# Small products in turn by array tile, the two heads of an attention pair in turn, and the latent keys of both heads in one product

## The chip, the cores and the metric

One Trainium2 chip, one core of it. The time is the device time of one execution in microseconds; lower is better. The core has a matrix engine (TensorE, PE in the profile, with its weight loads as PEld), a vector engine (VectorE, DVE), a scalar engine (ScalarE, ACT), GpSimd (POOL) and SyncE (SP), which issues the DMAs.

## What is computed

A two-layer backbone over 512 latent tokens and 256 context tokens, 1024 wide. In each layer a normalised and modulated stream goes through one input projection whose columns feed three groups of heads; their outputs are joined and projected back, and a SwiGLU block follows. Cut to what the change touches:

```python
# latent attention, 4 heads: keys and values from a 128-wide latent, a shared rotary part appended to each key
kv = (rms_norm(kvc, g_kv) @ w_kv_up).reshape(..., MLA_H, MLA_NOPE + MLA_V)
keys, vals = concat([ck, k]), concat([cv, v])        # context and latent tokens
out = softmax(q @ keys.T * scale) @ vals

# neighbourhood attention, 4 heads of 64, on an 8 x 64 grid, 16 columns around each query, and the context
p = softmax(concat([where(col_ok, q @ k_window.T * scale + bias, -inf), q @ ck.T * scale]))
o = p_loc @ v_window + p_ctx @ cv

# gated DeltaNet, 4 heads, two directions, chunks of 64: a unit lower triangular inverse per chunk and head
tinv = triangular_solve(L + eye, eye, lower=True, unit_diagonal=True)
u, w = tinv @ (v * beta), tinv @ (kb * exp(gc))
S_new = S * g_last + k_tail.T @ (u - w @ S)
```

## The kernel before, in words

All products are on TensorE. A product that has to be as good as fp32 at speed is split into a high and a low part and done as three products (`mm3`, line 107); other products take fp32 operands as they are, and the profile records each of those as two passes, a weight load and a matmul for each. `mm` (line 103, the call of the engine at line 104) is the one place from which nearly every product comes, so L104 says nothing about which it is; the names of the tiles do. The profile shortens names of tiles: pp64 is pp there, yq64 is yq, p32 and p64 are p, and Ys is strips.

The program is written as a sequence, and a framework puts each engine's instructions in an order of its own: ready work of several streams is interleaved on each engine, and the engine then runs its list in that order. Program order is the priority. Tiles come from rotating buffers: asking for a new one waits until the oldest of its tag has been read.

**Inverses.** `inverse(x0, sb, eb)` (line 916) makes the inverses for two chunks of 128 tokens, eight (chunk, head) pairs x. 32x32 blocks on the diagonal come ready from an earlier stage; the function joins them to 64x64 and then to 128x128. It has five groups of small products: pp (four 32-blocks b, eight x each; 32 products of 32x32, input mix), xq (blocks 1 and 2; 16 products of 32x32, input p), pp64 (two halves, 16 products of 64x64, input X), yq (32 products of 32x32, input strips), and yq64 (two halves, 16 products of 64x64, input Y). Block b lies on partitions 32b to 32b+31, which are rows of the array; its result goes to the partitions of block b^1 of one PSUM bank, or of b itself in xq. In each group the loop over blocks or halves is outside, that over x inside. There are three calls per layer: `inverse(0)` beside the last input projections, `I_(2)` and `I_(4)` as steps in the list `dn` beside the attentions.

**Neighbourhood attention.** `attention()` (line 847) is a generator; one `next` is one unit: a pair of heads and 128 queries. Layer 0 has 12 units (8 latent, 4 context), layer 1 has 8 latent ones. For each head j of the pair (its 64 dimensions on partitions 64j to 64j+63) a bank `s_` is taken, the scores of the window (256 columns, latent units only) and of the context (256 columns) are made with `mm3`, and then maximum (L870, L874), exponents (L877, L878), normalisation, four transposes (L889) and a copy (L891) follow. Then the value products of both heads fill one bank `o_`: for each block of 128 keys head 0, then head 1. The banks of tag S (scores) number two, those of tag T (transposes, values, accumulators) three.

**The list of steps beside it.** `beside()` (line 1099) takes steps from `dn` (scans and inverses) and, in layer 0, modulation columns from `ada_cols`, by the counts in `DNS` and `ADA`, before each unit of either attention; `TAIL` sets where the first units and the last projections stand. These lists are not changed.

**Latent attention.** For each pair of heads, head by head: query weights are loaded and split (`upw`, line 1138, one shared buffer wup), then the head's keys are made from 64 columns of `wkh`/`wkl` into bank `acc_mk`, 512 latent and 256 context columns, each evacuated by a cast (L1168, ACT) and a subtraction (L1169, DVE) into `kh`, `kl`; then its queries. Units of 128 queries follow, as in the neighbourhood attention; the value products (bank `o_mla`) go over the key blocks 0 to 5, for each of them head 0 and then head 1. The out-projection's first part is interleaved here by the framework.

Of the kernel before, what the change touches and what calls it, by code (L numbers as in the profile page):

```python
# [9 lines left out]
F32 = mybir.dt.float32  # L10
F32R = mybir.dt.float32r
AF = mybir.ActivationFunctionType
ALU = mybir.AluOpType
# [4 lines left out]
P = 128  # L18
# [344 lines left out]
def layer(tc, nc, a, l, es_x, xT, env, nx):  # L363
# [483 lines left out]
    def attention():  # L847
        for pair in range(2):
# [4 lines left out]
            for qt in range(nT // P):  # L853
# [5 lines left out]
                lo_ = 256 if is_ctx else 0  # L859
                pts = []  # L860
                for j in range(2):
                    hs = slice(64 * j, 64 * j + 64)
                    cutk = lambda t: grid(t)[hs, :, c0:c0 + 32].rearrange("p r (b c) -> p b r c", b=2)
                    s_ = att_bank("s_na")
                    if not is_ctx:
                        mm3(nc, s_[:, 0:256], (qh[hs, tok], ql[hs, tok]), (cutk(kh), cutk(kl)))
                    mm3(nc, s_[:, 256:512], (qh[hs, tok], ql[hs, tok]), (kh[hs, CTX], kl[hs, CTX]))
                    st_ = sn.tile([P, 8], F32, tag="st", name="st", bufs=4)
# [25 lines left out]
                for b in range(len(vb)):  # L894
                    for j in range(2):
                        hd = 2 * pair + j
                        mm(nc, o_[j * 64:j * 64 + 64, 0:P], nav[:, vb[b], hd * 64:hd * 64 + 64], pts[j][:, b * P:(b + 1) * P],
                           b == 0, b == len(vb) - 1)
# [17 lines left out]
    def inverse(x0, sb, eb):  # L916
# [14 lines left out]
        pp, xq = i8(q2[:, 0:256], 32), i8(q2[:, 256:512], 32)  # L931
        for b in range(4):
            o = b ^ 1
            for x in R8:
                mm(nc, pp[B4[o], x], LP[x // 4][B4[b], x % 4, B4[o]], mix[B4[b], x])
# [12 lines left out]
        S.copy(out=p32, in_=pp)  # L948
        for b in (1, 2):
            for x in R8:  # L950
                mm(nc, xq[B4[b], x], Ys[1 - b % 2][B4[b], x], p32[B4[b], x])
# [5 lines left out]
        hf = ((fst, snd), (snd, fst))  # L957
        for a_, b_ in hf:
            for x in R8:
                mm(nc, pp[b_, x], LP[x // 4][a_, x % 4, b_], Xh[a_, x])  # L960
# [3 lines left out]
        yq = i8(eb("yq")[:, 0:256], 32)  # L964
        for b in range(4):
            o = b ^ 1
            for x in R8:
                mm(nc, yq[B4[o], x], p32[B4[b], x], Ys[1 - b % 2][B4[b], x])
        for d, r, c in ((0, 0, 1), (0, 2, 3), (1, 1, 0), (1, 3, 2)):
            S.copy(out=Y[d][B4[r], :, c], in_=yq[B4[r]])  # L970
        yq = i8(eb("yq64"), 64)
        for d, (a_, b_) in enumerate(hf):
            for x in R8:
                mm(nc, yq[a_, x], p64[b_, x], Yf[d][b_, x, b_])
            S.copy(out=Yf[d][a_, :, b_], in_=yq[a_])
# [178 lines left out]
    for pair in range(2):  # L1154
        qk = []
        for j in range(2):
            hd = 2 * pair + j
            wqh, wql = upw(a["w_qup"][l, hd], 256, [(gq[:, i:i + 1], P * i, P * i + P) for i in range(2)], "wq")
            ws = slice(hd * 64, hd * 64 + 64)
            kh, kl = khl[j]  # L1160
            qh, ql = [sa.tile([P, T], F32R, tag=nm, name=nm, bufs=2) for nm in ("qh", "ql")]
            qf = sa.tile([P, T], F32, tag="pt", name="qf", bufs=2)
            q2 = sa.tile([P, T], F32, tag="pr", name="q2", bufs=2)
            for st_ in both:
                n = st_.stop - st_.start
                acc = att_bank("acc_mk")
                mm3(nc, acc[0:64, 0:n], (wkh[:, ws], wkl[:, ws]), (kvh[:, st_], kvl[:, st_]))
                S.copy(out=kh[0:64, st_], in_=acc[0:64, 0:n])  # L1168
                tt(out=kl[0:64, st_], in0=acc[0:64, 0:n], in1=kh[0:64, st_].bitcast(F32), op=ALU.subtract)  # L1169
            for st_ in sts:  # L1170
                n = st_.stop - st_.start
                acc = att_bank("acc_mq")
                for i in range(2):
                    w = slice(i * P, i * P + P)
                    mm3(nc, acc[:, 0:n], (wqh[:, w], wql[:, w]), (qll_[i][0][:, st_], qll_[i][1][:, st_]), i == 0, i == 1)
                S.copy(out=qf[0:64, st_], in_=acc[0:64, 0:n])
                tt(out=qf[64:96, st_], in0=acc[64:96, 0:n], in1=C("rope")[64:96, st_], op=ALU.mult)
                tt(out=q2[64:96, st_], in0=acc[96:128, 0:n], in1=C("rope")[96:128, st_], op=ALU.mult)
            dict(V=V, G=G)[next(eng, "G")].tensor_tensor(out=qf[64:96, :nT], in0=qf[64:96, :nT], in1=q2[64:96, :nT], op=ALU.add)
            split((qh[0:96, :nT], ql[0:96, :nT]), qf[0:96, :nT])  # L1180
            qk.append((kh, kl, qh, ql))
        for qt in range(nT // P):
# [38 lines left out]
            b0 = kst[0][1]  # L1221
            for b in range(b0, 6):
                for j in range(2):
                    hd = 2 * pair + j
                    mm(nc, o_[j * 64:j * 64 + 64, 0:P], vtok[:, b, hd * 64:hd * 64 + 64], pts[j][:, b * P:(b + 1) * P],
                       b == b0, b == 5)
            if pair:
# [239 lines left out]
```

## Time and profile before

| what | us |
|---|---|
| median of 3 runs | 2122.88 |
| lowest, highest | 2118.37, 2123.48 |
| profiled execution, its own time | 2125.45 |
| its span, first to last instruction | 2123.6 |
| TensorE's granted clock, mean | 0.968 |

The profile is of one execution. Busy time of an engine is the time covered by at least one of its instructions; matmuls are pipelined, so two records may overlap and a stream's records cover a little more than the time from its first start to its last. In a row of a timeline the first number is the start from the beginning of the span, the second the time covered, then engine, line, operation, out<-in, sizes and the number of records that were merged. For a matmul, 32*32 is the rows by columns of the array that it uses, 32x32 the partitions and columns that move.

### The profile page before, as it was taken

What the parts mean: (1) busy time and instruction counts of PE and PEld (TensorE: products, weight loads), DVE (VectorE), ACT (ScalarE), POOL (GpSimd) and SP (SyncE); (2) the same over time, 40 slices, a digit from 0 to 9 for tenths busy, and PEclk for the clock granted to TensorE, in tenths of its full rate; (3) what the DMA queues carried; (4) which work ended last, traced back from release to release, by engine and by line L of the source; (5) the groups of instructions that cost most, each with busy time, mean ns of one, the idle gap of its engine ahead of it and who ended that gap; (6) DMA issues with size and microseconds to landing.
All of it is one profiled execution on the core that took longest, in us unless ns stands there. A gap on an engine that the chain in (4) does not pass through costs nothing. (4 is left out here: it accounts for less than half of the span.)

```text
span 2123.6 us, 32023 instructions
## 1 busy us (share of the span) xinstructions
PE 1990.2 (94%) x12770; PEld 1684.4 (79%) x12770; DVE 1172.3 (55%) x2045; ACT 714.3 (34%) x1385; POOL 758.7 (36%) x540
## 2 busy tenths in 40 slices
PE   6999998998998999999999988888998889999998
PEld 4788787887787888888888876767787678888887
DVE  4888813667656457246443268894568753212123
ACT  5433322334544221122122244333434543222233
POOL 3466132104322222322222443823311353444444
PEclk9999998999999999999999999999999999999999
DMA  7324252543322345344442331334232231333332
GB/s 279 82 76 153 81 157 77 168 149 112 104 64 78 109 126 165 97 130 131 128 129 76 121 95 55 119 120 124 91 88 77 87 95 60 99 99 94 95 97 92
DMA packets 119309, 232.56 MB, mean 110 GB/s; under 512 B 30516, under 2 KB 55988, under 8 KB 119032
## 3 DMA queue, kind: packets, MB, share of 16 engines
q1 hardware_dynamic: 119160, 230.51, 34.9%
q8 instruction: 101, 1.65, 0.3%
q14 instruction: 48, 0.39, 0.1%
HBM read 199.46 MB, written 31.01 MB: 109 GB/s over the span
## 5 line engine op out<-in xcount | busy, mean ns | idle before, releaser
L217 POOL TENSOR_TENSOR wl<-wr,wh 128x1024 fp32r<-128x1024 f32 (+2 forms) x188 | 442.0, 2352 | 848.4 <-ACT wh L216 834.9
L216 ACT CAST wh<-wr 128x1024 fp32r<-128x1024 f32 (+2 forms) x190 | 193.5, 1019 | 713.0 <-PE acc_gu L104 287.6
L104 PE MATMUL acc_gu<-fh,wh 128*128 128x512 f32 (+1 forms) x1024 | 359.1, 353 | 9.5 <-ACT fh L304 8.7
L104 PE MATMUL acc_gu<-fl,wh 128*128 128x512 f32 (+1 forms) x1024 | 361.0, 353 | 4.1 <-DVE fl L305 4.1
L104 PE MATMUL acc_gu<-fh,wl 128*128 128x512 f32 (+1 forms) x1024 | 360.2, 352 | 0.0
L104 PE MATMUL acc_in<-hh,wh 128*128 128x512 f32 (+1 forms) x640 | 230.5, 364 | 18.6 <-ACT xp L491 6.9
L104 PE MATMUL acc_in<-hl,wh 128*128 128x512 f32 (+1 forms) x640 | 229.9, 360 | 3.2 <-DVE hl L305 2.0
L104 PE MATMUL acc_in<-hh,wl 128*128 128x512 f32 (+1 forms) x640 | 227.3, 359 | 3.4 <-POOL wl L217 3.4
L104 PEld LDWEIGHTS acc_gu<-fh,wh 128*128 128x128 f32 x1024 | 194.1, 190 | 37.5 <-ACT fh L304 10.9
L1348 DVE TENSOR_TENSOR av<-acc_gu,av 128x768 f32<-128x768 f32 (+1 forms) x44 | 36.3, 825 | 338.4 <-PE acc_gu L104 330.0
L104 PEld LDWEIGHTS acc_gu<-fl,wh 128*128 128x128 f32 x1024 | 195.0, 190 | 30.3 <-DVE fl L305 4.3
L104 PEld LDWEIGHTS acc_gu<-fh,wl 128*128 128x128 f32 x1024 | 194.9, 190 | 26.3
L104 PEld LDWEIGHTS acc_in<-hh,wh 128*128 128x128 f32 x640 | 126.1, 198 | 45.4 <-ACT xp L491 8.6
L104 PE MATMUL acc_d<-al,wh 128*128 128x512 f32 (+1 forms) x444 | 157.2, 354 | 0.0
L104 PE MATMUL acc_d<-ah,wh 128*128 128x512 f32 (+1 forms) x444 | 157.2, 354 | 0.0
L104 PE MATMUL acc_d<-ah,wl 128*128 128x512 f32 (+1 forms) x444 | 156.1, 354 | 0.0
L254 DVE CUSTOM_DVE_ANT_0 junk<-wada,scb 128x1024 f32<-128x1024 f32 x112 | 145.3, 1297 | 6.8 <-DMA wada<-w_adaT 4.0
L104 PEld LDWEIGHTS acc_in<-hl,wh 128*128 128x128 f32 x640 | 127.0, 198 | 25.2 <-DVE hl L305 4.6
L104 PEld LDWEIGHTS acc_in<-hh,wl 128*128 128x128 f32 x640 | 126.1, 198 | 22.8 <-POOL wl L217 4.7
L1366 DVE SCALAR_TENSOR_TENSOR xT<-acc_d,mod,xT 128x512 f32<-128x512 f32 (+1 forms) x76 | 46.5, 634 | 155.2 <-PE acc_d L104 155.2
L501 DVE SCALAR_TENSOR_TENSOR cy<-xp,cw,cy 128x770 f32<-128x770 f32 (+1 forms) x96 | 117.7, 1226 | 20.5 <-ACT cy L499 18.5
L1352 DVE TENSOR_TENSOR al<-av,ah 128x768 fp32r<-128x768 f32 (+1 forms) x44 | 100.4, 2282 | 35.1 <-ACT ah L1351 35.1
(391 smaller groups left out, 3857.0 us busy)
## 6 DMA issues: line engine op xcount, KB each, us to landing
wr<-w_gu SPq DMA_DIRECT2D x88, 512.0 KB, 3.5
wada<-w_adaT SPq DMA_DIRECT2D x56, 512.0 KB, 3.4
wr<-w_in SPq DMA_DIRECT2D x48, 512.0 KB, 3.6
wr<-w_dn SPq DMA_DIRECT2D x32, 448.0 KB, 3.3
wada<-w_ada SPq DMA_DIRECT2D x24, 512.0 KB, 3.4
wada<-w_ada SPq DMA_DIRECT2D x8, 1024.0 KB, 8.1
wr<-w_dn SPq DMA_DIRECT2D x16, 512.0 KB, 3.5
xT<-xT SPq DMA_DIRECT2D x16, 384.0 KB, 4.9
```

What stands on the lines that cost most here:

```text
L104: nc.tensor.matmul(out, lhsT, rhs, start=start, stop=stop)
L216: S.copy(out=hi[:, sl], in_=raw[:, sl])
L217: eng.tensor_tensor(out=lo[:, sl], in0=raw[:, sl], in1=hi[:, sl].bitcast(F32), op=ALU.subtract)
L254: V.tensor_tensor_reduce(out=junk, in0=w, in1=scb[:, s], scale=1.0, scalar=0.0, op0=ALU.mult, op1=ALU.add, accum_out=mod[l][:, part, j, s: ...
L501: stt(out=y[:, :wid], in0=xp[:, j:j + wid], scalar=w_(j), in1=y[:, :wid], op0=ALU.mult, op1=ALU.add)
L1348: tt(out=av[:, :nT], in0=accs[1][:, :nT], in1=av[:, :nT], op=ALU.mult)
L1352: after.append(tt(out=l_[:, :nT], in0=av[:, :nT], in1=h_[:, :nT].bitcast(F32), op=ALU.subtract))
L1366: stt(out=xT[:, m, st_], in0=acc, scalar=mod[l][:, 5, m, s:s + 1], in1=xT[:, m, st_], op0=ALU.mult, op1=ALU.add)
```

## The change

Four things. In `inverse` the loops are exchanged in all five groups: x outside, blocks or halves inside (the copies of yq64 follow after both halves). In `attention` both banks of a unit are taken first, and each of the three products of `mm3` is issued for head 1 and then head 0 before the next; the sums are the same. In both attentions the value products go head 1 first for each block; in the latent attention the context blocks 4 and 5 come before 0 to 3. The keys of both heads of a pair come from one product of 128 columns, ahead of both heads' query weights, and each head's half is evacuated by its own cast and subtraction.

```diff
-                pts = []
+                pts, ss = [], [att_bank("s_na") for j in range(2)]
+                hs = [slice(64 * j, 64 * j + 64) for j in range(2)]
+                cutk = lambda t, j: grid(t)[hs[j], :, c0:c0 + 32].rearrange("p r (b c) -> p b r c", b=2)
+                trio = ((qh, kh), (qh, kl), (ql, kh))
+                if not is_ctx:
+                    for i, (q_, k_) in enumerate(trio):
+                        for j in (1, 0):
+                            mm(nc, ss[j][:, 0:256], q_[hs[j], tok], cutk(k_, j), i == 0, i == 2)
+                for i, (q_, k_) in enumerate(trio):
+                    for j in (1, 0):
+                        mm(nc, ss[j][:, 256:512], q_[hs[j], tok], k_[hs[j], CTX], i == 0, i == 2)
                 for j in range(2):
-                    hs = slice(64 * j, 64 * j + 64)
-                    cutk = lambda t: grid(t)[hs, :, c0:c0 + 32].rearrange("p r (b c) -> p b r c", b=2)
-                    s_ = att_bank("s_na")
-                    if not is_ctx:
-                        mm3(nc, s_[:, 0:256], (qh[hs, tok], ql[hs, tok]), (cutk(kh), cutk(kl)))
-                    mm3(nc, s_[:, 256:512], (qh[hs, tok], ql[hs, tok]), (kh[hs, CTX], kl[hs, CTX]))
+                    s_ = ss[j]
...
                 for b in range(len(vb)):
-                    for j in range(2):
+                    for j in (1, 0):
...
-        for b in range(4):
-            o = b ^ 1
-            for x in R8:
+        for x in R8:
+            for b in range(4):
+                o = b ^ 1
                 mm(nc, pp[B4[o], x], LP[x // 4][B4[b], x % 4, B4[o]], mix[B4[b], x])
...
-        for b in (1, 2):
-            for x in R8:
+        for x in R8:
+            for b in (1, 2):
                 mm(nc, xq[B4[b], x], Ys[1 - b % 2][B4[b], x], p32[B4[b], x])
...
-        for a_, b_ in hf:
-            for x in R8:
+        for x in R8:
+            for a_, b_ in hf:
                 mm(nc, pp[b_, x], LP[x // 4][a_, x % 4, b_], Xh[a_, x])
...
-        for b in range(4):
-            o = b ^ 1
-            for x in R8:
+        for x in R8:
+            for b in range(4):
+                o = b ^ 1
                 mm(nc, yq[B4[o], x], p32[B4[b], x], Ys[1 - b % 2][B4[b], x])
...
+        for x in R8:
+            for d, (a_, b_) in enumerate(hf):
+                mm(nc, yq[a_, x], p64[b_, x], Yf[d][b_, x, b_])
         for d, (a_, b_) in enumerate(hf):
-            for x in R8:
-                mm(nc, yq[a_, x], p64[b_, x], Yf[d][b_, x, b_])
             S.copy(out=Yf[d][a_, :, b_], in_=yq[a_])
...
     for pair in range(2):
         qk = []
+        ws = slice(pair * P, pair * P + P)
+        for st_ in both:
+            n = st_.stop - st_.start
+            acc = att_bank("acc_mk")
+            mm3(nc, acc[:, 0:n], (wkh[:, ws], wkl[:, ws]), (kvh[:, st_], kvl[:, st_]))
+            for j in range(2):
+                kh, kl = khl[j]
+                S.copy(out=kh[0:64, st_], in_=acc[64 * j:64 * j + 64, 0:n])
+                tt(out=kl[0:64, st_], in0=acc[64 * j:64 * j + 64, 0:n], in1=kh[0:64, st_].bitcast(F32), op=ALU.subtract)
         for j in range(2):
...
-            for st_ in both:
-                n = st_.stop - st_.start
-                acc = att_bank("acc_mk")
-                mm3(nc, acc[0:64, 0:n], (wkh[:, ws], wkl[:, ws]), (kvh[:, st_], kvl[:, st_]))
-                S.copy(out=kh[0:64, st_], in_=acc[0:64, 0:n])
-                tt(out=kl[0:64, st_], in0=acc[0:64, 0:n], in1=kh[0:64, st_].bitcast(F32), op=ALU.subtract)
...
-            for b in range(b0, 6):
-                for j in range(2):
+            bs_ = (4, 5, 0, 1, 2, 3)[:6 - b0]
+            for b in bs_:
+                for j in (1, 0):
                     hd = 2 * pair + j
                     mm(nc, o_[j * 64:j * 64 + 64, 0:P], vtok[:, b, hd * 64:hd * 64 + 64], pts[j][:, b * P:(b + 1) * P],
-                       b == b0, b == 5)
+                       b == 4, b == bs_[-1])
```

## Rows read from the trace of the kernel before

**Rows 1.** The page, engines: busy us, share of the span, instructions.

```profile
PE 1990.2 (94%) x12770; PEld 1684.4 (79%) x12770; DVE 1172.3 (55%) x2045; ACT 714.3 (34%) x1385; POOL 758.7 (36%) x540
```

**Rows 2.** Stretches, us: length, busy time per engine, granted clock, DMA share, GB/s.

```profile
290.00:350.00 60.00, 55.81 (x483) 47.87 (x481) 11.47 (x19) 17.76 (x32) 15.91 (x10) 0.95 0.31 99
350.00:490.00 140.00, 133.75 (x1556) 112.79 (x1556) 92.12 (x290) 45.30 (x150) 26.66 (x28) 0.93 0.49 155
490.00:553.00 63.00, 53.09 (x361) 44.08 (x361) 49.60 (x112) 33.24 (x112) 21.35 (x29) 0.89 0.18 53
...
1525.00:1590.00 65.00, 61.80 (x778) 54.67 (x779) 43.88 (x110) 23.71 (x70) 16.52 (x13) 0.95 0.31 94
1590.00:1678.00 88.00, 75.69 (x556) 63.30 (x556) 70.19 (x150) 40.50 (x129) 24.65 (x34) 0.96 0.24 69
```

**Rows 3.** Stretches of 0.1 us, PE records of pp alone.

```profile
295.37:295.47 0.10, 0.10 (x9) 1.00 0.20 82
...
296.36:296.46 0.10, 0.10 (x13) 1.00 0.00 0
```

**Rows 4.** Timeline of PE, a unit of the neighbourhood attention's scores.

```profile
388.24 0.29 PE L104 MATMUL s_na<-nkl,nqh 64*128 64x256 f32 x2
388.36 0.29 PE L104 MATMUL s_na<-nkh,nql 64*128 64x256 f32 x2
388.49 0.28 PE L104 MATMUL s_na<-nkh,nqh 64*128 64x256 f32 x1
388.61 0.28 PE L104 MATMUL s_na<-nkl,nqh 64*128 64x256 f32 x1
```

**Rows 5.** Groups on PE, 290 to 350: count | busy us, mean ns | idle before.

```profile
L104 PE MATMUL yq<-Y,p 64*64 64x64 f32 x32 | 2.3, 221 | 0.0
L104 PE MATMUL pp<-mix,LP 32*32 32x32 f32 x64 | 1.9, 192 | 0.0
L104 PE MATMUL yq<-strips,p 32*32 32x32 f32 x64 | 1.9, 192 | 0.0
L104 PE MATMUL pp<-X,LP 64*64 64x64 f32 x32 | 1.9, 221 | 0.0
...
L104 PE MATMUL pp<-p,strips 32*32 32x32 f32 x32 | 1.1, 192 | 0.0
```

**Rows 6.** Eight stretches summed, PE: s_na, o_na, o_mla, acc_mk, in this order.

```profile
sum 690.00, PE 34.47; mean PE 4.31
...
sum 690.00, PE 27.86; mean PE 3.48
...
sum 690.00, PE 36.59; mean PE 4.57
...
sum 690.00, PE 10.98; mean PE 1.37
```

**Rows 7.** Timeline of PE, value products of one unit.

```profile
370.78 0.69 PE L104 MATMUL o_na<-pt,nav 128*64 128x128 f32 x2
...
371.89 1.09 PE L104 MATMUL o_na<-pt,nav 128*64 128x128 f32 x14
```

**Rows 8.** Records of two tiles: count, ns min/median/max, first and last start us, forms.

```profile
L104 PE MATMUL o_na<-pt,nav x288: 272/273/475, 370.8 to 1583.4; 128*64 128x128 f32 x144
...
L1169 DVE TENSOR_TENSOR kl<-acc_mk,kh x16: 406/545/684, 499.8 to 1660.7; 64x512 fp32r<-64x512 f32 x8, 64x256 fp32r<-64x256 f32 x8
```

**Rows 9.** Timeline, exponents of one unit's heads and the next unit's first score.

```profile
383.08 0.45 ACT L878 ACTIVATE pr<-s_na,st 128x256 f32<-128x256 f32 x1
...
384.02 0.46 ACT L878 ACTIVATE pr<-s_na,st 128x256 f32<-128x256 f32 x1
...
386.58 0.38 PE L104 MATMUL s_na<-nkh,nqh 64*128 64x256 f32 x1
```

**Rows 10.** An idle stretch of PE, and the stretch at the low clock there.

```profile
358.94 0.59 PE L104 MATMUL tr_ada<-cst,adarow 128*128 128x2 f32 x2 [3.79 <-DVE adarow L231]
...
358.10:371.80 13.70, 12.85 (x64) 10.93 (x64) 7.13 (x27) 5.48 (x18) 1.04 (x1) 0.50 0.17 46
```

More of the change, by code (lines that the diff above doesn't have):

```diff
@@ L1158, in layer @@
             wqh, wql = upw(a["w_qup"][l, hd], 256, [(gq[:, i:i + 1], P * i, P * i + P) for i in range(2)], "wq")
-            ws = slice(hd * 64, hd * 64 + 64)
             kh, kl = khl[j]
```

## The prediction

> **What bounds the kernel now.** I read the page's engine list first: TensorE (PE) is busy 1990.2 of 2123.6 us, VectorE (DVE) 1172.3 [rows 1]. A busy share is an average over stages, so the table by stretch comes next. In the stretches that hold the inverses and the neighbourhood attention PE is busy 55.81 of 60, 133.75 of 140 and 61.80 of 65 us; DVE is far lower, 92.12 of 140 and 43.88 of 65 [rows 2]. Only in the two in which the latent attention starts does PE stand idle for 10 of 63 and 12 of 88 us [rows 2]. So up to there, time taken from PE is time taken from the stage, as long as the softmax and scan chains beside it keep up.
>
> Then: does PE use the whole array in that time? It does not, and where two streams happen to meet the trace already shows what the change would do.
>
> - Products of 32x32. In the middle of one block's run nine passes touch a tenth of a microsecond; where one block gives way to the next it is thirteen [rows 3]. A record lasts 0.19 us, so the starts counted fall into 0.10 + 0.19 = 0.29 us: one per 32 ns against one per 22 ns. Passes of one tile follow each other at 32 ns; those of the next tile start in between.
> - Scores of two heads. At 388.24 one product of each head runs: two records cover 0.29 us where a single one lasts 0.28, and the next pair follows 0.12 us later. The single ones behind them also step by 0.12 us [rows 4]. Two heads together cost what one costs.
>
> In both, the products lie on different rows of the array (partitions 0 to 63 against 64 to 127, or different groups of 32). In program order the kernel does eight products of one tile, or all of one head, before the other.
>
> **The change, part by part.** Savings are PE time first.
>
> (a) Inverses. Each of the six has 112 small products, recorded as two passes each. In the undisturbed one the five groups cover 1.9 (mix), 1.1 (p), 1.9 (X), 1.9 (strips) and 2.3 us (Y, two separate halves) [rows 5]. Off each run goes the last record's tail, 0.19 us (0.22 for 64x64, both the groups' means). mix and strips: 1.71 us for 64 passes becomes 16 steps of 32 ns on four tiles, 0.51: 1.2 saved each. p: 0.91 on two tiles becomes 0.51: 0.4 saved. Y: a half takes 2.3/2 - 0.22 = 0.93; both together take one half's time, and one switch of stream goes: 1.0 saved. X: 1.68 becomes such a run of 0.93: 0.75 saved. Sum 1.2 + 1.2 + 0.4 + 1.0 + 0.75 = 4.6 us, times six = 27 us. Four row tiles at once stand in no row; two at once would save half of mix and strips less (0.8 instead of 1.2 each), 22 us in all. I take four, since two tiles show no slowing of either.
>
> A page speaks against this. The Trainium skill (TensorE: Matmul & The Clock Gate, Part 1, "Wait — 56ns, not 53.3ns?") says that starts never come closer than about 25 ns however small the product. By that, an estimate from the page's figure, mix, strips and p would save 0.1 us each and (a) 6 x (0.3 + 0.75 + 1.0) = 12 us. The trace does not agree: 22 ns over a stretch of which only a part overlaps [rows 3], and pairs within 0.01 us [rows 4].
>
> What waits: with x outermost the first step needs all four transposes of mix instead of one, and the copies of Y's first half wait for both halves. PE has projections or attention queued beside them [rows 2], so I cost this at nothing; without that cover, some 1 us an inverse (one half of Y, 0.93).
>
> (b) Neighbourhood scores. 16 latent units have six products per head, four context units three: 16 x 6 + 4 x 3 = 108 pairs at 0.12 us saved [rows 4] = 13 us. The records cover 34.47 us [rows 6]; half of that, 17 us, is the ceiling (it has low clock and switches of stream in it). Some pairs are there already [rows 4]; none kept would be 0. I take 13. Against it both banks are now taken before a unit's first product, and head 1's comes first: the slower rival.
>
> (c) Value products, head 1 first. Today head 0's first product runs alone as soon as its probabilities are there (two passes), the other fourteen follow after other work in 1.09 us [rows 7]. Those fourteen are one lone pass, six pairs and a lone one: eight steps. Sixteen in pairs are eight steps too. So the separate run goes, 0.69 us [rows 7] less a record's tail of 0.27 [rows 8] = 0.42 us for a unit split like this. There are 20 units in each attention: 16 us if all are split, 0 if none; the records cover 27.86 and 36.59 us [rows 6]. I take half, 8 us. Context blocks first in the latent attention I cost at nothing: a run can't end before both copies of the probabilities have landed.
>
> (d) Keys of both heads in one product. 48 products become 24 with as many moving columns; the records cover 10.98 us [rows 6], half is 5. Against it: a bank is held over four evacuations instead of two, and in program order head 0's query weights (a DMA issue on SyncE, two scalings on DVE, a cast on ACT, a subtraction on DVE or POOL) and its queries come behind head 1's keys, two DVE subtractions and two casts more: 2 x 0.545 = 1.1 us [rows 8] at each of four pair starts. Scans and out-projection cover it where PE has them. Bounds: 5 gained, 4 lost. I take 2 gained.
>
> PE sum: 27 + 13 + 8 + 2 = 50 us.
>
> **What of it arrives.** About 32 of the 50 us lie in 350 to 490 and 1525 to 1590, 205 us with PE idle for 9.5, or 5% [rows 2]. With less PE work there, the chains (softmax over DVE and ACT, the scan's state) show more; the latent attention, with fewer PE streams, has 14 to 16% idle [rows 2]. Halfway, 10% of the 173 us left is 17 instead of 9.5: 7 or 8 lost. The granted clock goes with it: 0.93 in the busy stretch, 0.89 in the thin one [rows 2]; 0.02 of 173 us is 3 more. So 50 - 10 = 40 us arrive.
>
> The span is 2123.6, the profiled execution's own time 2125.45, the median of the runs 2122.88, 2.6 us less. I take the difference off the median: 2122.9 - 40 = 2083 us.
>
> **The rivals.**
> - *The chains take over.* The unit's chain (maximum, exponent, normalise, transpose, copy, values) and the scan set the pace. For: a unit's last exponent starts at 384.02 and ends near 384.5, the next unit's products come at 386.58 [rows 9]; 2.1 us of slack, not more. Against: DVE is at 66%. Then (b) and (c) are lost inside the stage, and what stays is the inverses in the projection stretches (2 x 4.6) and half of the other four (9): 18 us, 2105.
> - *The order doesn't hold.* PE's issue order is not the program's: the values of one unit already stand in two pieces [rows 7]. If the two heads' products are pulled apart, (b) brings 4 and (c) nothing: 33 less 7 for idle, 26 us, 2097.
> - *Starts come no closer than seen.* At 22 ns a pass, mix and strips save 0.3 each, p 0.2: (a) is 6 x (0.8 + 1.0 + 0.75) = 15, the sum 38, less 7: 31 us, 2092. The skill's page named above would make it 2095.
> - *Slower: the score banks become a stall.* Place: a unit's first product, now head 1's, whose bank is freed last. Head 1's exponent starts 0.94 us after head 0's [rows 9]; PE is in order, and what is queued behind that product waits too. 20 x 0.94 = 19 us alone don't decide. It decides if the stall grows so long that the clock falls: after 3.79 us of idle it was granted at 0.50 for 13.7 us [rows 10], so 3.8 + 13.7/2 = 10.7 us each time. Four such eat the 40 us; six make it 64 - 40 = 24 us slower, 2147. Against: the products now come 2.1 us after both banks are free.
>
> **How the numbers follow.** Forecast 0.61, its own range 2066 (all of (c), 17 in (b), 5 lost: 57) to 2098 (two tiles at once, (d) at its loss, 15 for the chains: 25). Chains 0.17, order 0.08, starts 0.05, stall 0.05, and 0.04 for a gain beyond, with less low clock than now. A measurement tells 0.3%, 6.4 us, from no change. Of the chains 0.04 and of sums that cancel 0.02 lie within: same 0.06, slower 0.05, faster 0.89. The range that leaves out no more than 2 in 10: 2064 to 2110.
>
> **What would show it.** Right: mix and strips covering about 0.7 us instead of 1.9; scores in pairs throughout, covering near 20 us; values in one run per unit; 24 key products; 350 to 490 some 20 us shorter with PE idle under 15. Wrong: starts of four tiles 22 ns or more apart; PE idle before the scores, released by head 1's exponent; more low clock in these stretches; scores still single.

## The result, and the profile after

The changed kernel took 2097.76 us (median of 4 runs, 2095.13 to 2100.99) against 2122.14 for the kernel before (4 runs): a ratio of 0.9885, 95% interval 0.9862 to 0.9907. The gain is 24 us where 40 were forecast; the time lies inside the range. The profiled execution after had 2095.13 us, the lowest of its four; that of before was 3 us above the median of its own. So the two profiles differ by 30 us where the medians differ by 24.

First the page's engine line, after:

```profile
PE 1939.7 (93%) x12746; PEld 1644.8 (79%) x12746; DVE 1177.3 (56%) x2045; ACT 714.2 (34%) x1385; POOL 761.6 (36%) x540
```

Against [rows 1] PE is busy 1990.2 - 1939.7 = 50.5 us less. The forecast's sum of saved PE time was 50. So PE was relieved as foreseen, and 20 of the 50 us did not reach the end. Where they went is read from matching stretches: neighbourhood attention of layer 0 (from the last product of the input projection to the last value product), its latent attention with the out-projection (from there to the first product of the SwiGLU block), layer 1's stretch from its first input projection to its first neighbourhood score, its neighbourhood attention, its latent attention with the out-projection. Columns as in [rows 2]: length, busy PE, PEld, DVE, ACT, POOL, granted clock, DMA share, GB/s. Before:

```profile
344.10:484.20 140.10, 132.18 (x1537) 111.61 (x1537) 91.98 (x289) 44.13 (x149) 26.24 (x29) 0.93 0.48 151
484.20:669.90 185.70, 165.29 (x1085) 136.49 (x1081) 123.40 (x266) 85.47 (x227) 65.57 (x54) 0.95 0.25 81
...
1225.70:1428.40 202.70, 173.64 (x906) 139.67 (x904) 161.37 (x232) 79.78 (x132) 103.31 (x100) 0.94 0.32 98
1428.40:1583.40 155.00, 145.00 (x1390) 123.80 (x1391) 85.55 (x219) 60.42 (x143) 40.93 (x27) 0.93 0.33 95
1583.40:1740.60 157.20, 142.96 (x1001) 120.05 (x1000) 108.02 (x227) 71.15 (x193) 52.36 (x50) 0.98 0.30 90
```

The same stretches after:

```profile
335.80:462.80 127.00, 118.84 (x1597) 102.88 (x1597) 95.70 (x299) 43.73 (x158) 29.88 (x35) 0.96 0.57 176
462.80:647.50 184.70, 155.37 (x1012) 129.59 (x1008) 119.30 (x255) 85.84 (x218) 62.47 (x47) 0.92 0.24 75
...
1202.10:1412.00 209.90, 178.33 (x920) 143.18 (x918) 167.46 (x241) 80.31 (x134) 104.62 (x100) 0.93 0.31 95
1412.00:1550.30 138.30, 126.82 (x1426) 107.37 (x1426) 83.36 (x213) 60.16 (x143) 41.39 (x27) 0.94 0.37 108
1550.30:1711.60 161.30, 140.98 (x941) 119.08 (x940) 108.30 (x224) 71.13 (x191) 53.46 (x50) 0.94 0.28 86
```

Three readings follow.

- **The neighbourhood attentions got most of what was promised.** They are 140.1 - 127.0 = 13.1 and 155.0 - 138.3 = 16.7 us shorter, and PE stands idle there as little as before: 7.9 + 10.0 us before, 8.2 + 11.5 after. The stretch ahead of the first lost 8.3 us (344.1 to 335.8). All six inverses lie in these three stretches.
- **The stretch ahead of the second, which holds none of the changed products, is 7.2 us longer**: 202.7 to 209.9. But it doesn't hold the same work. Counted in the traces by their starts, 26 products of `acc_v` and 240 DVE instructions lie in it, 13 and 231 before; the difference stood behind the first score. So part of the 16.7 us is the other side of these 7.2. Taken together the two are 9.5 us shorter, with 13.5 us less for PE to do.
- **The latent attentions gave nothing.** In layer 0 PE has 9.9 us less to do, stands idle for 29.3 instead of 20.4 us, and the granted clock falls from 0.95 to 0.92: 1.0 us is gained. In layer 1 PE has 2 us less to do, and the stretch is 4.1 us longer, at 0.94 instead of 0.98.

Now the parts. (a), the groups of the undisturbed inverse after, which answer to [rows 5], from the view of groups on PE (count | busy us, mean ns | idle before):

```profile
L104 PE MATMUL pp<-X,LP 64*64 64x64 f32 x32 | 1.5, 223 | 0.0
L104 PE MATMUL yq<-Y,p 64*64 64x64 f32 x32 | 1.1, 221 | 0.0
L104 PE MATMUL yq<-strips,p 32*32 32x32 f32 x64 | 1.0, 194 | 0.0
L104 PE MATMUL pp<-mix,LP 32*32 32x32 f32 x64 | 0.8, 194 | 0.0
L104 PE MATMUL pp<-p,strips 32*32 32x32 f32 x32 | 0.7, 192 | 0.0
```

9.1 us have become 5.1: 4.0 saved where 4.6 were forecast. X and strips run into each other here, which costs both some tenths; mix, alone, went from 1.9 to 0.8.

(b) and (c), the timeline of PE after, one unit's scores, its neighbour's, and two units' values:

```profile
357.47 1.09 PE L104 MATMUL o_na<-pt,nav 128*64 128x128 f32 x16
360.16 0.38 PE L104 MATMUL s_na<-nkh,nqh 64*128 64x256 f32 x1
360.38 0.28 PE L104 MATMUL s_na<-nkl,nqh 64*128 64x256 f32 x1
360.50 0.28 PE L104 MATMUL s_na<-nkh,nql 64*128 64x256 f32 x1
360.62 0.28 PE L104 MATMUL s_na<-nkh,nqh 64*128 64x256 f32 x1
...
363.23 0.38 PE L104 MATMUL s_na<-nkh,nqh 64*128 64x256 f32 x1
363.45 0.28 PE L104 MATMUL s_na<-nkl,nqh 64*128 64x256 f32 x1
...
369.12 1.09 PE L104 MATMUL o_na<-pt,nav 128*64 128x128 f32 x16
```

Values come in one run of sixteen records that lasts 1.09 us, as forecast: the separate run of [rows 7] is gone. Scores are still mostly single: one head's six products at 360.16, the other's at 363.23, 3 us later. The program asks for pairs; the framework's order puts other work between the heads. It isn't a wait for a bank: the exponents that read the two banks last start one after the other, at 357.95 and 359.30, and the second ends at 359.79, ahead of both heads' products. That the framework orders head by head because it expects the banks one after the other is argued, not shown.

What the products cover on PE after, against [rows 6], in its order s_na, o_na, o_mla, acc_mk (the stretches summed, here and in [rows 6], hold all of them but the very first unit's scores, about 1 us):

```profile
sum 750.00, PE 30.64; mean PE 15.32
...
sum 750.00, PE 20.97; mean PE 10.49
...
sum 750.00, PE 31.05; mean PE 15.53
...
sum 750.00, PE 5.44; mean PE 2.72
```

Scores 34.47 to 30.64, 3.8 saved; values 27.86 to 20.97 and 36.59 to 31.05, 12.4 saved; keys 10.98 to 5.44, 5.5 saved. The inverses' two tiles pp and yq, summed in the same way, went from 60.5 to 34.5 us, 26 saved. Together 48 of the 50.5. Of these, 26 + 3.8 + 6.9 = 37 lie ahead of the latent attentions, in the stretches that together got 8.3 + 13.1 + 9.5 = 31 us shorter: there most of the PE time turned into time. The other 11 lie in the latent attentions and did not.

### The profile page after: what moved, and what is told of

Same layout as the page of the kernel before. It is cut to its first block, busy times and chain, and to the rows that moved or that the text cites. A ratio compares the mean times of both kernels' runs of the same rounds, so it can differ in the third digit from the quotient of the medians.

```text
span 2093.4 us, 32000 instructions
## 1 busy us (share of the span) xinstructions
PE 1939.7 (93%) x12746; PEld 1644.8 (79%) x12746; DVE 1177.3 (56%) x2045; ACT 714.2 (34%) x1385; POOL 761.6 (36%) x540
## 5 line engine op out<-in xcount | busy, mean ns | idle before, releaser
L104 PE MATMUL acc_in<-hh,wh 128*128 128x512 f32 (+1 forms) x640 | 228.3, 360 | 20.4 <-ACT xp L491 8.5
L104 PE MATMUL acc_d<-al,wh 128*128 128x512 f32 (+1 forms) x444 | 157.2, 354 | 0.0
L104 PE MATMUL acc_d<-ah,wh 128*128 128x512 f32 (+1 forms) x444 | 157.2, 354 | 0.0
```

What stands on the lines that cost most here:

```text
L104: nc.tensor.matmul(out, lhsT, rhs, start=start, stop=stop)
```

## The experiments

The theory: PE time is paid back where PE sets the pace, and (d) takes some away, since the keys of head 1 now stand ahead of head 0's queries on ACT, DVE and in the banks. Rivals: (b) or (c) costs something of its own; or nothing in particular does, and the framework's new order of the instructions around the change moves the time. Where an expectation speaks of the place of the keys (theory P), the first of these is meant.

**The inverses alone.** All five loop exchanges and nothing else; one of them:

```diff
-        for b in range(4):
-            o = b ^ 1
-            for x in R8:
+        for x in R8:
+            for b in range(4):
+                o = b ^ 1
                 mm(nc, pp[B4[o], x], LP[x // 4][B4[b], x % 4, B4[o]], mix[B4[b], x])
...
```

> Only the five loops of the inverses are exchanged. Theory A (PE time is what counts in the projection and neighbourhood stretches; there most of it arrives): inverse products cover 31 us instead of 56, and 15 to 21 us of the 25 come out in the time, ratio 0.990 to 0.993. Rival B (everything that PE saves arrives everywhere): 25 us, ratio 0.988. Rival C (the framework's new order of the instructions, not the overlap, makes the time): the products cover the same 31 us but the ratio is anywhere between 0.995 and 1.002.

Measured: 2106.18 against 2121.23 us, ratio 0.9934 (0.9915 to 0.9953), 14 us gained. On PE they cover 35.5 us, nearly as in the whole change. They bring more than half of the whole gain and less than the 22 to 27 of the forecast. The profiled execution is the slowest of the six, 2114.93 us. In it the three stretches with the inverses are 27 us shorter, and two without any are longer: that of the second reading above by 8.4 us (202.7 to 211.1, with the same 13 products moved into it), layer 1's latent attention by 12.7 (157.2 to 169.9).

**The scores alone.** Both banks first, head 1 and head 0 in turn, nothing else:

```diff
-                    s_ = att_bank("s_na")
-                    if not is_ctx:
-                        mm3(nc, s_[:, 0:256], (qh[hs, tok], ql[hs, tok]), (cutk(kh), cutk(kl)))
...
+                pts, ss = [], [att_bank("s_na") for j in range(2)]
...
+                    for i, (q_, k_) in enumerate(trio):
+                        for j in (1, 0):
+                            mm(nc, ss[j][:, 0:256], q_[hs[j], tok], cutk(k_, j), i == 0, i == 2)
```

> Only the scores of the neighbourhood attention, both banks taken first, heads in turn. Theory A (the two banks come free one after the other, so the framework issues head by head and few pairs form): cover of the score records 28 to 32 us instead of 34, ratio 0.997 to 1.001. Rival B (they pair): cover near 20 us, ratio 0.994. Rival D (the score banks become a stall): PE idle before scores, released by the exponent, grows by over 5 us, ratio over 1.003.

Measured: 2125.41 against 2121.23, ratio 1.0018 (1.0006 to 1.0031). Nothing gained. The records cover 30.22 us, 4 less than before.

**The values alone.** The order of the value products in both attentions:

```diff
-                    for j in range(2):
+                    for j in (1, 0):
...
-            for b in range(b0, 6):
-                for j in range(2):
+            bs_ = (4, 5, 0, 1, 2, 3)[:6 - b0]
+            for b in bs_:
+                for j in (1, 0):
```

> Only the order of the value products in both attentions. Theory A (the split runs go, some 10 us of PE; half of it in the neighbourhood attention arrives, that in the latent attention turns into idle): cover of o_na 21 to 23 and of o_mla 31 to 33 us, ratio 0.996 to 0.999. Rival B (all arrives): 10 us, ratio 0.995. Rival E (waiting for head 1 costs as much as pairing brings): ratio 1.000.

Measured: 2125.23, ratio 1.0027 (1.0012 to 1.0042). Values cover 51.7 us instead of 64.5, 12.8 of PE time saved, and the end is if anything later.

**The keys alone.** One product for both heads, ahead of both heads' queries:

```diff
+        for st_ in both:
+            n = st_.stop - st_.start
+            acc = att_bank("acc_mk")
+            mm3(nc, acc[:, 0:n], (wkh[:, ws], wkl[:, ws]), (kvh[:, st_], kvl[:, st_]))
+            for j in range(2):
...
         for j in range(2):
             hd = 2 * pair + j
             wqh, wql = upw(a["w_qup"][l, hd], 256, [(gq[:, i:i + 1], P * i, P * i + P) for i in range(2)], "wq")
...
-            for st_ in both:
-                n = st_.stop - st_.start
-                acc = att_bank("acc_mk")
-                mm3(nc, acc[0:64, 0:n], (wkh[:, ws], wkl[:, ws]), (kvh[:, st_], kvl[:, st_]))
```

> Only the keys of both heads in one product. Theory A (PE waits at the pair starts anyway, and head 0's queries come later): key products cover 5 us instead of 11, ratio 0.999 to 1.003. Rival B (all arrives): 5 us less, ratio 0.9975. If the longer hold of the banks costs more than the products, PE idle and low clock in the latent attention grow and the ratio is over 1.003.

Measured: 2130.0, ratio 1.0041 (1.0027 to 1.0056), 9 us lost. The forecast's bounds for (d) were 5 gained and 4 lost.

The four ratios alone add up to 0.2% slower; together the parts are 1.15% faster. So they don't add, and the next runs take one part away from the whole.

**The whole change with its pairs held.** Each score product of a unit is tied behind the one before it, so that the framework can't issue one head ahead:

```diff
+                prev = None
+                for o2_, l_, r_, s0_, s1_ in todo:
+                    with tc.issue_after(prev.ins) if prev is not None else ExitStack():
+                        prev = PE.matmul(o2_, l_, r_, start=s0_, stop=s1_)
```

> The changed kernel with PE's order of one unit's score products chained: head 1's first product, then head 0's, and so on, so that no later score product is issued before its partner. Theory A (the scores did not pair because their banks come free one after the other, and pairing them is worth its PE time less what the first product now waits): cover of the score records 18 to 22 us instead of 29, time 3 to 8 us below the changed kernel. Rival D (waiting for both banks is a stall): cover as low, but PE idle before scores up by 5 us or more and the time the same as the changed kernel's or longer.

Measured: 2093.15 against 2119.96, ratio 0.9877 (0.9856 to 0.9898). Counted in the traces, the two heads' products start within 30 ns of each other in 21 of 108 pairs before, in 37 after, and in 93 here. In the timeline (the product's line is L873 in this kernel):

```profile
364.92 0.40 PE L873 MATMUL s_na<-nkh,nql 64*128 64x256 f32 x2
365.04 0.39 PE L873 MATMUL s_na<-nkh,nqh 64*128 64x256 f32 x2
365.17 0.39 PE L873 MATMUL s_na<-nkl,nqh 64*128 64x256 f32 x2
```

Pairs follow each other at 0.12 us, the pace of single ones in [rows 4], and the cover, summed as above, falls to 25.29 us: 9.2 less than before, not 13. So the price of a pair was right and the order was what failed. The time gains little: the interval overlaps that of the changed kernel.

**The whole change with the old scores.** The scores as before, all else changed.

```diff
-                pts, ss = [], [att_bank("s_na") for j in range(2)]
...
+                    s_ = att_bank("s_na")
+                    if not is_ctx:
+                        mm3(nc, s_[:, 0:256], (qh[hs, tok], ql[hs, tok]), (cutk(kh), cutk(kl)))
```

> The changed kernel with the old scores (head by head, a bank at a time); inverses, values and keys as changed. Theory A (the score part brought little): within 4 us of the changed kernel. Rival B: 9 us or more above it.

Measured: 2094.54, ratio 0.9877 (0.9859 to 0.9894). (b) as it was written brings nothing in company either.

**The whole change with the old keys.** The keys head by head in front of each head's queries, as before; the diff is that of the keys alone, the other way round.

```diff
-            mm3(nc, acc[:, 0:n], (wkh[:, ws], wkl[:, ws]), (kvh[:, st_], kvl[:, st_]))
...
+                mm3(nc, acc[0:64, 0:n], (wkh[:, ws], wkl[:, ws]), (kvh[:, st_], kvl[:, st_]))
```

> The changed kernel with the old keys (one product per head); the rest as changed. Theory A (the key part brings nothing, since the latent attention waits on its chains): within 4 us of the changed kernel, either side, with PE idle in the latent attention lower than there. Rival B: 5 us above it.

Measured: 2079.43 (2078.71 to 2085.91), ratio 0.9815 (0.9792 to 0.9838). The best time of all. The changed kernel was run once more beside it, without an edit:

> The changed kernel once more, beside the three above, so that they are compared on one chip: 2095 to 2101 us, ratio 0.987 to 0.990.

Measured: 2098.31, ratio 0.9896 (0.9878 to 0.9914). So the keys cost 0.81%, 17 us, in company: nearly half of what the change would otherwise bring. In this second profile of the same kernel PE is busy for 1946.1 us instead of 1939.7, and the score records cover 32.80 us instead of 30.64, so sizes of a few us read from one profile are rough.

**Pairs held, old keys.** Both edits above at once.

```diff
+                        prev = PE.matmul(o2_, l_, r_, start=s0_, stop=s1_)
...
+                mm3(nc, acc[0:64, 0:n], (wkh[:, ws], wkl[:, ws]), (kvh[:, st_], kvl[:, st_]))
```

> Chained score pairs together with the old keys; inverses and values as changed. If the parts add (keys cost 19 us beside the others, the chain brought 5): 2072 to 2077 us, ratio 0.977 to 0.980. If the chain's gain was only an accident of the order: 2077 to 2085.

Measured: 2088.74 against 2121.31, ratio 0.984 (0.982 to 0.986). Neither range on record was met. Holding the pairs, which gave 0.2% with the merged keys, costs 0.25% here; the intervals overlap both times, so neither is clear of the noise. The score records cover 25.32 us, as with the merged keys. Between this kernel and the whole change with its pairs held (0.9877) the keys are the only difference. By the ratios they cost 0.37%, 8 us, though these intervals overlap a little too.

**Old products, new place.** One key product per head as before, but both heads' keys ahead of the queries. This tells the place from the merging:

```diff
-            mm3(nc, acc[:, 0:n], (wkh[:, ws], wkl[:, ws]), (kvh[:, st_], kvl[:, st_]))
+        for j in range(2):
+            ws = slice((2 * pair + j) * 64, (2 * pair + j) * 64 + 64)
...
+                mm3(nc, acc[0:64, 0:n], (wkh[:, ws], wkl[:, ws]), (kvh[:, st_], kvl[:, st_]))
```

> The changed kernel with one key product per head as before, but both heads' keys ahead of both heads' queries, as in the change. Theory P (the place of the keys costs: head 0's queries and their evacuations come behind head 1's keys on ACT and DVE): as slow as the changed kernel, 2094 to 2102 us. Theory H (the hold costs: the merged product's two banks are kept over four evacuations each, so the third bank alone serves the queries): as without the key part, 2077 to 2085 us. In between if both count.

Measured: 2091.71, ratio 0.9853 (0.9829 to 0.9877). That is between the ranges of the two theories.

**New product, other place.** The merged product as it is, but behind head 0's query products:

```diff
+            for st_ in both if j == 0 else ():
+                n = st_.stop - st_.start
+                ws = slice(pair * P, pair * P + P)
+                acc = att_bank("acc_mk")
+                mm3(nc, acc[:, 0:n], (wkh[:, ws], wkl[:, ws]), (kvh[:, st_], kvl[:, st_]))
```

> The changed kernel with the merged key product moved behind head 0's query products (ahead of their rotation and split). Theory P: head 0's queries are no longer late, 2077 to 2087 us. Theory H: the hold is the same, 2093 to 2102 us.

Measured: 2083.16, ratio 0.9814 (0.9795 to 0.9834). That is in the range of the place. The merged product costs nothing against the old keys' 0.9815 when it stands there; unmerged keys in the new place go half of the way to the changed kernel, though their interval overlaps the old keys' a little.

**Inverses and scores alone.** Old keys, old order of the values.

```diff
-                    for j in (1, 0):
+                    for j in range(2):
...
```

> Inverses and scores as changed; keys and values as before. Beside the run without keys alone (2079 us) it tells what the value order brings in company. Theory A (half of its 10 us of PE arrives): 2082 to 2087 us. Rival B (all arrives): 2088 to 2092. Theory C (the framework's new order decides, as for the parts alone): 2070 to 2081 or over 2093, with the latent attention's stretches no shorter with the value order than without it.

Measured: 2080.2 (2076.85 to 2089.32) against 2121.63, ratio 0.9803 (0.979 to 0.9816). The same as with the values, so (c) is worth nothing that these runs can tell. Against the inverses alone (0.9934) the scores add 1.3% here, some 27 us, though they save at most 4 us of PE time and brought nothing alone or beside the merged keys. Most of these 27 us can't be PE time of the scores: the order that the framework comes to is worth as much as the keys are.

**What the keys' place does**, in the timeline. First the changed kernel, layer 0's first pair, from the first key product to the first product that needs the low part of head 0's queries:

```profile
477.81 0.50 PE L104 MATMUL acc_mk<-kvh,wkh 128*128 128x512 f32 x1 [0.23 <-ACT vtok L1162]
...
480.15 0.58 ACT L1173 CAST kh<-acc_mk 64x512 fp32r<-64x512 f32 x1 [0.39 <-DVE kl L1174]
...
482.30 0.36 PE L104 MATMUL acc_mq<-ql0h,wqh 128*128 128x256 f32 x1 [0.68 <-DVE kl L1174]
...
489.94 0.57 PE L104 MATMUL s_mla<-kh,qh 96*128 96x512 f32 x1 [1.83 <-ACT qh L1137]
...
491.62 2.12 DVE L1138 TENSOR_TENSOR ql<-qf,qh 96x768 fp32r<-96x768 f32 x1
...
493.79 1.01 PE L104 MATMUL s_mla<-kh,ql 96*128 96x512 f32 x2 [2.42 <-DVE ql L1138]
```

Then the same with the old keys and all else changed:

```profile
479.92 0.44 PE L104 MATMUL acc_mk<-kvh,wkh 128*64 128x512 f32 x1 [0.23 <-ACT vtok L1162]
...
482.39 0.28 PE L104 MATMUL acc_mq<-ql0h,wqh 128*128 128x256 f32 x1
...
489.07 0.46 PE L104 MATMUL s_mla<-kh,qh 96*128 96x512 f32 x1
...
490.31 0.94 DVE L1138 TENSOR_TENSOR ql<-qf,qh 96x768 fp32r<-96x768 f32 x1
...
491.37 0.59 PE L104 MATMUL s_mla<-kh,ql 96*128 96x512 f32 x2
```

With the keys ahead head 1's cast waits for a subtraction, head 0's context queries wait 0.68 us for the bank that a subtraction `kl` still reads, and the scores 1.83 and 2.42 us for `qh` and `ql`. 16.0 us pass, against 11.4. Not all of the 4.6 us between them is the order: 1.2 is the subtraction for `ql` itself, which lasts 2.12 us here and 0.94 there. A GpSimd addition into `qf` (491.12, 1.80 us) runs beside it here, and begins only after it there (492.29); whether that slows it was not tried, and with the old keys it lasted up to 2.02 us in other kernels. The granted clock falls with the idle time: in the ten microseconds around these waits PE is busy for 5.93 at a granted 0.51, after

```profile
480.00:490.00 10.00, 6.60 (x42) 4.99 (x40) 7.49 (x16) 5.00 (x10) 4.19 (x4) 1.00 0.25 70
490.00:500.00 10.00, 5.93 (x15) 3.92 (x16) 9.04 (x17) 3.82 (x15) 5.70 (x8) 0.51 0.06 21
```

and with the old keys for 7.00 at 0.66:

```profile
482.00:492.00 10.00, 8.45 (x53) 6.75 (x51) 9.06 (x19) 4.71 (x10) 4.22 (x4) 1.00 0.22 66
492.00:502.00 10.00, 7.00 (x25) 6.09 (x26) 8.99 (x22) 5.70 (x21) 5.62 (x7) 0.66 0.09 27
```

The whole in one table, for all fourteen profiles: this same time summed over the four pair starts; the two latent attentions with their out-projections; the stretch of layer 1 that holds none of the changed products; and that stretch with the neighbourhood attention behind it. For the merged keys behind head 0's queries a pair start is counted from the first query product, which comes first there. The profiles of the inverses alone and of inverses and scores are some 9 us above their kernels' medians.

| kernel | four pair starts, us | latent attentions, us | stretch of layer 1, us | with its neighbourhood attention, us |
|---|---|---|---|---|
| before | 49.2 | 342.8 | 202.7 | 357.7 |
| inverses alone | 50.8 | 353.0 | 211.1 | 353.3 |
| scores alone | 51.8 | 344.2 | 211.9 | 360.4 |
| values alone | 52.7 | 343.1 | 210.7 | 358.1 |
| inverses and scores | 53.1 | 342.0 | 202.8 | 338.8 |
| changed, old keys | 49.4 | 327.6 | 210.9 | 347.6 |
| pairs held, old keys | 52.6 | 344.6 | 211.0 | 343.7 |
| keys alone | 55.3 | 352.0 | 202.5 | 357.1 |
| changed, first and second profile | 58.5, 57.7 | 346.0, 342.0 | 209.9, 208.6 | 348.2, 348.7 |
| changed, pairs held | 58.4 | 345.8 | 210.5 | 345.5 |
| changed, old scores | 60.5 | 347.5 | 209.7 | 342.2 |
| unmerged keys ahead | 62.5 | 341.3 | 210.8 | 349.3 |
| merged keys behind head 0's queries | 47.5 | 341.1 | 203.2 | 335.5 |

The pair starts sort by the place of the keys alone: 49 to 53 us in the seven kernels with the old keys, 55 to 63 in the six profiles with the keys ahead, 47.5 with them behind. Merged or not makes no difference of that kind. That the place lengthens the starts, by some 7 us (means 51.4 and, of the five with the merged product, 58.1), is shown.

That these 7 us are what the keys cost is not shown. The latent attentions, in which the starts lie, do not sort with them: 342 to 353 us in six kernels with the old keys, 341 to 352 in the six profiles with the keys ahead, 341 with them behind. With the keys alone they are 9.2 us longer than before (352.0 against 342.8), and in the changed kernel 14 to 18 us longer than with the old keys (346.0 and 342.0 against 327.6); but that 327.6 is 14 us or more under every other kernel with the old keys. With the pairs held the two kinds of keys differ there by 1.2 us. And the kernel with the longest starts, 62.5, is no slower than the changed one (0.9853 against 0.9896). So the times show that the keys as written cost something, alone and in company; what makes the cost stays open. The last rival, a new order around the change and nothing in particular, is not excluded: the 27 us that the scores added to the inverses are of that kind, and larger than the keys' 17.

The stretch of layer 1 sorts by nothing that was edited: 202.5 to 203.2 in four kernels, 208.6 to 211.9 in ten profiles, and none between. Two kernels of a single part, both with only attention code edited, the keys alone and the scores alone:

```profile
1225.80:1428.30 202.50, 176.31 (x908) 141.51 (x906) 159.66 (x229) 79.64 (x132) 102.71 (x100) 0.94 0.32 99
```

```profile
1223.30:1435.20 211.90, 177.82 (x918) 142.72 (x916) 168.24 (x241) 80.18 (x134) 104.95 (x100) 0.93 0.31 94
```

PE has within 1.5 us the same to do and stands idle 8 us longer in the second, where DVE has 9 us more work in the stretch. What differs is what stands in the stretch: in all ten longer ones 26 products of `acc_v` and 239 or 240 DVE instructions come ahead of the first score, in the four shorter ones 13 and 230 or 231, and the others follow it. So an edit anywhere can make the framework put instructions elsewhere, and the length of a stretch tells of that too. With the neighbourhood attention behind it (last column) the two kernels are 3 us apart, not 9. Something of it may stay in the time: among the kernels with the changed inverses the two with the shorter stretch have 335.5 and 338.8 there, the others 342 to 353. Why the order changes was not tried. The gain of the merged keys behind the queries lies there too: against the changed kernel's second profile, 5.4 us in this stretch and 7.8 in the neighbourhood attention after it, under one in the latent attentions. So that run shows that the product can be merged at no loss, not that its place gave the 0.8%.

## Why the prediction was right and wrong

- **What bounds the kernel: right.** In layer 0's neighbourhood attention 13.1 us less time for 13.3 us less PE work (132.18 - 118.84), in layer 1's, with the stretch ahead of it, 9.5 for 13.5, with PE in both attentions nearly as rarely idle as before.
- **(a): right.** 27 us of PE time forecast, 26 measured. Four tiles do run at once. The mark named, "mix and strips covering about 0.7 us instead of 1.9", came for mix (0.75 in the timeline), while strips, mixed with X, took 1.0. Less the last record's 0.19, mix's 64 passes start in 0.56 us, one per 9 ns. The sentence of the Trainium skill that spoke against it (TensorE: Matmul & The Clock Gate, Part 1, "Wait — 56ns, not 53.3ns?"), read as a rule for different tiles too, would have them start no closer than some 25 ns, 64 x 25 = 1.6 us by an estimate from that figure; for different tiles this trace does not agree. In time (a) brought 14 us by itself, 41 with the scores; in its one profile the stretches with the inverses gained 27 and others lost, layer 1's latent attention above all.
- **(b): the size was wrong.** 13 us forecast, 3.8 measured, and 1.7 in the changed kernel's second profile. The step that failed is that the program's order would hold. It was on record as a rival ("order doesn't hold", (b) brings 4) and its figure, 2097, is the time measured; but not by its sum, since there (c) brought nothing and PE saved 33 us, where in fact it saved 50. That the figure fits is luck. In time (b) brought nothing alone or beside the merged keys and 27 us on top of the inverses, far more than its PE time. The framework's order pulls the pair apart, in the unit shown with both banks free; why it does is open.
- **(c): PE time right and low, its worth wrong.** 8 us forecast, 12.4 measured on PE, in one run per unit as said; in time nothing, alone or in company. The term went into the sum as if all PE time were alike. 5.5 of it lie in the latent attentions, which got no shorter; for the 6.9 in the neighbourhood attentions the runs with and without (c), 2079.43 and 2080.2, show no difference either, and why is open.
- **(d): the sign was wrong.** 2 us gained forecast; measured, 9 lost alone and 17 in company (8 with the pairs held, not clear of the noise). The PE half, 5.5 saved, came true to the half microsecond. What failed is the other half, the price of the place: "two DVE subtractions and two casts more: 2 x 0.545 = 1.1 us [rows 8] at each of four pair starts". It counted the subtractions' own time only, 4 us in four starts. The casts run on another engine ahead of head 0's, the wait for a bank and the low clock after the idle time come on top: the starts got 7 us longer. And the cover named for it, scans and out-projection, didn't hold: PE idles at these starts. That is still under the cost, and the latent attentions as a whole don't follow the starts, so where the cost comes from is open, and the order around the change may be all of it.
- **What arrives: half right.** Of 50 us 10 were taken off, 7 or 8 for idle time and 3 for the clock, all worked out on the neighbourhood attentions. Up to their end 31 of 37 us arrived, so there the loss was no larger than allowed for. What the sum left out is the latent attentions: PE had 12 us less to do there, and they are 3 us longer in this profile and 0.9 shorter in the second.
- **The other rivals.** The chains didn't take over: PE idle in the neighbourhood attentions rose by 1.7 us, and by 2.5 in the stretch ahead of layer 1's. Starts came closer than any seen before. The slower case, a stall at the score banks, didn't come. In the view of PE's waits (tile waited in, line, releaser: us in total, times, longest us), before:

```profile
PE s_na L104 <- ACT pr L878: 3.6, 3, 1.9
```

and after:

```profile
PE s_mla L104 <- DVE ql L1138: 4.4, 4, 2.4
...
PE s_na L104 <- ACT pr L885: 2.7, 4, 1.9
```

The wait for the exponents that free the score banks fell from 3.6 to 2.7 us. A wait that is new stands in the latent attention, for `ql`.

The best kernel found keeps (a), (b) and (c) and the old keys: 2079.43 us, 1.9% under the kernel before. That inverses and scores alone reach the same 2080 says that not much of it hangs on (c). Part of the figure may be the order that the framework happened on: with pairs held the same keys gave 2089, and no other kernel had so short latent attentions.

## What to carry to other kernels

Small products on different tiles of the array should be issued in turn, tile by tile: here it took their cover from 60.5 to 34.5 us, and where the matrix engine sets the pace most of it came out in the time. Before two products are merged, look at what their evacuations stand in front of: here the merged keys saved 5.5 us of PE time and cost 17 us ahead of the first head's queries, for a reason that stayed open, and nothing behind them. Where a framework orders the instructions, don't count on a pair because the program asks for it: read in the trace whether it is one, and hold it explicitly if it is worth that. Judge a part by several kernels with and without it, and count what a stretch holds before its length is compared: here one stretch grew by 4% because other work had moved into it.

## What the runs showed of the hardware that was not expected

Passes of 32x32 on four row tiles, each writing other partitions of one PSUM bank, start 9 ns apart on the average, where one tile's own passes keep 32 ns [rows 3]; a quarter of that is 8, so the four hardly slow each other. Two tiles of 64x64 cover 1.1 us for 32 passes: less the record's 0.22, 0.88 for 16 steps, 55 ns a step, the pace of one alone (0.93 for 16 in a half before).
